# A written order for the ramp of a one-core attention block: load, norm, transposes and first projection

## The chip, the cores and the metric

One core of a Trainium2 chip runs the whole program. The metric is device time in microseconds (us), median of several runs of the same program; lower is better. Engines: PE (TensorE, products and transposes), DVE (VectorE), ACT (ScalarE), POOL (GpSimd), SP (its queue issues the large DMAs).

## The reference

One layer over x of 256 tokens by 1024, fp32:

```python
h = rmsnorm(x, norm_mix)
proj = h @ w_in                       # 9 * 512 + 8 + 3 * 1024 columns
q_a, k_a, v_a, q_b, k_b, v_b, f_b, q_c, k_c, v_c, g = split(proj)
o_a = stick_breaking_attention(q_a, k_a, v_a)      # 8 heads of 64 each
o_b = forgetting_attention(q_b, k_b, v_b, f_b + b_forget)
o_c = moba_attention(q_c, k_c, v_c, alibi slopes)  # one block here: causal + ALiBi
mixed = sum_n sigmoid(g[n]) * (o_n @ w_branch[n])
x = x + mixed @ w_out
x = x + relu(rmsnorm(x, norm_mlp) @ w_up) ** 2 @ w_down
return rmsnorm(x, norm_final)
```

Every product is made to near fp32 precision from halves: each operand is split into a rounded part "hi" (type fp32r) and the rest "lo" = value - hi, and three products hi\*hi, lo\*hi and hi\*lo are added up in PSUM.

## The kernel before, in words

The weights (75.5 MB by their shapes) stream through SBUF in 1 MB units, listed in `plan` (L72 to L83) in the order of use: q, k, v of branch a, and so on, then gates, lifts, out, up, down. `pump` (L88) converts them: for each unit one DMA into a "raw" buffer (two of these, tag `raw`; SP queue, L95), then in halves hi = copy (ACT, L107) and lo = raw - hi (DVE, L110). Up to 7 halves lie ahead of their use (`HALVES`); `used` (L117) counts a half as consumed and pumps the next. The first unit, q of branch a, is an exception: its halves are two DMAs of 512 KB (`raw0`, L103), and its hi parts `whi_qa` are made on POOL (L109), lo of half 0 on DVE and lo of half 1 on POOL (L110).

Before the first product the kernel loads x (two tiles of 128 tokens, L154) and runs 12 products on zeros (`pw`, L172). Each tile is normalised: sum of squares on ACT and DVE (L185, L186), power -1/2 on POOL (`rstd`, L199), scaling to `h` on DVE and ACT (L224, L225). PE transposes the 16 128x128 blocks (`ptr`, L205), and each of the 8 blocks of features k becomes, times the norm's gain, `hT`: hi by ACT (L210) and lo by DVE (L212). Constants for the attention masks are made on POOL and DVE (L240 to L269): `zeros`, `minus`, `neg_past`, `neg_tri`, `neg_ones` (a cast on DVE, L249), `identr` (L251), `rel`, `sel`, `neg_sel`, `ones_row`.

`proj_first` (L306) makes q of branch a: 48 products of 128x128 by 256 columns into two PSUM tiles (j = 0, 1), in six runs of 8 over k, named (j, a, b): a picks hi or lo of the weights, b hi or lo of `hT`. Order: (0,0,0), (1,0,0), (0,1,0), (0,0,1), (1,0,1), (1,1,0). `qk_split` (L281) then writes q as hi and lo into zero-padded tiles (`pad_hi`, `pad_lo`). After it come k of branch a (`proj_qk`, 48 products), the 16 products `pf` of the forget gate (`forget_terms`, L435; weights `raw_f` and `wf`), v of branch a (`proj_v`), and the rest: attention steps interleaved with further projections, gates, lifts, output projection, MLP.

What sets the order of instructions: the text goes through a planner, which simulates the program with costs of its own and lists the instructions of each engine as they come ready in its simulation; each engine then executes its list in order. So the order on an engine need not be that of the text: L249 and L251 are written behind L212 and run ahead of it on DVE.

Of the kernel before, what the change touches and what calls it, by code (L numbers as in the profile page):

```python
# [24 lines left out]
EPS = 1e-6  # L25
WARM = 12
LO = 32
ROOT_D = 32.0
# [9 lines left out]
def hybrid_attention_block(ctx, tc, x, norm_mix, w_in, b_forget, w_branch, w_out,  # L38
# [48 lines left out]

    def pump():  # L88
        while state["next"] < min(2 * len(plan), state["used"] + HALVES):
            n, i = divmod(state["next"], 2)  # L90
# [8 lines left out]
            if n:  # L99
                raw = state["raw"][part]  # L100
            else:
                raw = act.tile([P, a, b], F32, name="raw0", tag=("v_hi", "v_lo")[i], bufs=2)
                nc.sync.dma_start(raw, src[part])  # L103
            hi = wp.tile([P, a, b], F32R, name=f"whi_{which}{br}{j}{i}", tag="whi", bufs=HALVES)
# [12 lines left out]
    def used(n=1):  # L117

        state["used"] += n
        pump()  # L120
# [40 lines left out]

    ident = const.tile([P, P], F32, name="ident")
    make_identity(nc, ident)
    minus_half = const.tile([P, 1], F32, name="minus_half")
    nc.gpsimd.memset(minus_half, -0.5)

# [7 lines left out]

    pg = ps.tile([P, 2 * KD], F32, name="pg", tag="dense", bufs=3)
    nc.tensor.transpose(pg, gains, ident[0:2 * KD, 0:2 * KD])
    g_col = const.tile([P, 2 * KD], F32, name="g_col")
    nc.vector.tensor_scalar(g_col[:, 0:KD], pg[:, 0:KD], ROOT_D, None, op0=ALU.mult)
    nc.vector.tensor_copy(g_col[:, KD:], pg[:, KD:])
    g_mix, g_mlp = g_col[:, 0:KD], g_col[:, KD:2 * KD]  # L180

    def square_sum(src, junk, ss):

        n = src.shape[-1] // 2
        nc.scalar.activation(junk[:, 0:n], src[:, 0:n], AF.Square, accum_out=ss[:, 0:1])  # L185
        nc.vector.tensor_tensor_reduce(junk[:, n:], src[:, n:], src[:, n:], 1.0, 0.0, ALU.mult, ALU.add, ss[:, 1:2])  # L186

    def total_square(src, junk, so_far=D * EPS):


        ss = small.tile([P, 2], F32, name="ss", tag="ss")
        square_sum(src, junk, ss)
        total = small.tile([P, 1], F32, name="total", tag="total")
        made = nc.vector.scalar_tensor_tensor(total, ss[:, 0:1], so_far, ss[:, 1:2], op0=ALU.add, op1=ALU.add)
        return total, made

    def rsqrt(ms):
        rstd = small.tile([P, 1], F32, name="rstd", tag="rstd")
        nc.gpsimd.tensor_tensor(rstd, ms, minus_half, op=ALU.pow)  # L199
        return rstd  # L200

    def transposes(h, t, k0, pt):

        for i in range(2):
            nc.tensor.transpose(pt[:, i, t], h[:, (k0 + i) * P:(k0 + i + 1) * P], ident)  # L205

    def split_gain(pt, k0, g, hi, lo):
        src = [pt[:, i].rearrange("p t q -> p (t q)") for i in range(2)]
        for i, k in enumerate((k0, k0 + 1)):
            nc.scalar.activation(hi[:, k], src[i], AF.Copy, scale=g[:, k:k + 1])  # L210
        for i, k in enumerate((k0, k0 + 1)):
            nc.vector.scalar_tensor_tensor(lo[:, k], src[i], g[:, k:k + 1], hi[:, k].bitcast(F32),  # L212
                                           op0=ALU.mult, op1=ALU.subtract)

    def ptr(tag):
        return ps.tile([P, 2, NT, P], F32, name="ptr", tag=tag, bufs=3 if tag == "dense" else None)

    hT = keep.tile([P, KD, 2, S], F32R, name="hT", tag="hT")
    h_hi, h_lo = hT[:, :, 0], hT[:, :, 1]
    hs = []  # L220
    for t in range(NT):
        h = act.tile([P, D], F32, name="h", tag="pad_lo", bufs=2)
        rstd = rsqrt(total_square(x_sb[t], h)[0])
        nc.vector.tensor_scalar(h[:, 0:512], x_sb[t][:, 0:512], rstd, None, op0=ALU.mult)  # L224
        nc.scalar.activation(h[:, 512:], x_sb[t][:, 512:], AF.Copy, scale=rstd)  # L225
        hs.append(h)
    for k0 in range(0, KD, 2):
        pt = ptr("po" if k0 == 2 else "dense")
        for t in range(NT):
            transposes(hs[t], t, k0, pt)  # L230
        split_gain(pt, k0, g_mix, h_hi, h_lo)
    pump()


# [27 lines left out]
    sel = act.tile([LO, H, P], F32, name="sel", tag="v_hi", bufs=2)  # L262
    nc.gpsimd.memset(sel, -1.0)
    neg_sel = act.tile([LO + H, H, P], F32R, name="neg_sel")
    for j, n in ((0, LO), (LO, H)):
        nc.gpsimd.affine_select(neg_sel[j:j + n], sel[0:n], pattern=[[1, H], [0, P]], compare_op=ALU.is_equal,
                                fill=0.0, base=0, channel_multiplier=-1)
    ones_row = act.tile([H, S], F32, name="ones_row")
    nc.gpsimd.memset(ones_row, 1.0)  # L269


# [21 lines left out]
    def proj_qk(which, br, quad):  # L293

        padded = (which == "q") == (br == "a")
        for j in range(2):
# [7 lines left out]
            yield  # L304

    def proj_first():  # L306
# [162 lines left out]
    def forget_bias(pair):  # L469
# [3 lines left out]
        for s in range(2):  # L473
            h = 2 * pair + s
            nc.tensor.matmul(pb[:, s], neg_sel[:, h], parts, start=True, stop=True)
        for s in range(2):
# [254 lines left out]
```

## Time and profile before

| | us |
|---|---|
| median of 3 runs | 471.01 (469.85 to 471.64) |
| profiled execution, time | 471.74 |
| its span, first to last instruction | 470.0 |
| PE busy in the span | 456.7 (97%) |
| DVE busy | 328.2 (70%) |
| ACT busy | 274.1 (58%) |
| POOL busy | 42.1 (9%) |
| mean granted PE clock | 0.993 of full speed |

Times in the profile are from the start of the span. An engine's row merges neighbouring instructions of one kind: its length is that of the merged stretch, and in brackets stands the idle time ahead of it and whose end ended it. Busy time of PE is modelled and pipelined: products overlap, so the distance between their starts is what counts. Matmuls run at 2.4 GHz where the granted clock is 1.00 and at 1.2 GHz where it is 0.50.

### The profile page before, as it was taken

The page shows a single profiled execution, that of the slowest core. Times are in us where ns is not written, and L with a number is a line of the kernel's source. Part 1 is how long each engine was busy: PE and PEld are TensorE (multiplying, and loading weights), DVE is VectorE, ACT ScalarE, POOL GpSimd, SP SyncE. Part 2 cuts the span into 40 slices and gives each one's busy share as a digit, 9 for nine tenths or more (in the row PEclk, how much of TensorE's full clock was granted, in tenths as well). Part 3 has the DMA queues.
Part 4 walks back from the last instruction along what each step waited for, and adds up shares of the span by engine and source line. Part 5 has one row for each costly group of instructions (what it writes and reads, how often), then busy time and mean ns, then how long its engine had stood idle before and what let it go on. Part 6 is the DMA issues. An engine that isn't in the chain of part 4 may idle for free. (4 is left out here: it accounts for less than half of the span.)

```text
span 470.0 us, 6865 instructions
## 1 busy us (share of the span) xinstructions
PE 456.7 (97%) x2583; PEld 394.9 (84%) x2583; DVE 328.2 (70%) x544; ACT 274.1 (58%) x474; POOL 42.1 (9%) x79
## 2 busy tenths in 40 slices
PE   6999999999999999999999998999999999999993
PEld 3888998899899888888888887888888888888882
DVE  3987787778878877758858848987788744444425
ACT  6358898777767696556556436566555543334302
POOL 3910111132100001000000000000000000000012
PEclk9899999999999999999999999999999999999998
DMA  8377344343345448655555626776665555555202
GB/s 287 86 263 259 119 157 146 122 142 129 120 149 164 139 144 276 217 181 179 181 180 179 190 79 189 223 214 184 186 196 200 201 199 178 181 178 179 90 1 89
DMA packets 56834, 79.65 MB, mean 169 GB/s; under 512 B 2385, under 2 KB 44641, under 8 KB 56801
## 3 DMA queue, kind: packets, MB, share of 16 engines
q1 hardware_dynamic: 56464, 78.81, 52.0%
q8 instruction: 20, 0.33, 0.3%
q10 hardware_dynamic: 336, 0.40, 0.2%
q14 instruction: 14, 0.11, 0.1%
HBM read 78.16 MB, written 1.05 MB: 169 GB/s over the span
## 5 line engine op out<-in xcount | busy, mean ns | idle before, releaser
L110 DVE TENSOR_TENSOR wlo_d<-raw,whi_d 128x1024 fp32r<-128x1024 f32 x32 | 39.2, 1226 | 41.5 <-ACT whi_d L107 41.5
L136 PE MATMUL pu<-h,whi_u 128*128 128x512 f32 x256 | 64.7, 393 | 1.2 <-DVE h L212 1.2
L107 ACT ACTIVATE whi_d<-raw 128x1024 fp32r<-128x1024 f32 x32 | 33.9, 1061 | 50.5 <-PE ptok L136 42.4
L136 PEld LDWEIGHTS pu<-h,whi_u 128*128 128x128 f32 x256 | 45.9, 189 | 9.8 <-DVE h L212 1.5
L107 ACT ACTIVATE whi_u<-raw 128x1024 fp32r<-128x1024 f32 x32 | 33.5, 1060 | 29.7 <-PE pu L136 14.8
L136 PE MATMUL ptok<-whi_d,u_lo 128*128 128x512 f32 x128 | 50.5, 395 | 0.0
L136 PE MATMUL ptok<-whi_d,u_hi 128*128 128x512 f32 x128 | 50.5, 395 | 0.0
L110 DVE TENSOR_TENSOR wlo_u<-raw,whi_u 128x1024 fp32r<-128x1024 f32 x32 | 39.0, 1223 | 15.4 <-ACT whi_u L107 15.3
L136 PE MATMUL pg<-hT,whi_g 128*128 128x512 f32 x192 | 48.3, 393 | 0.0
L136 PEld LDWEIGHTS pg<-hT,whi_g 128*128 128x128 f32 x192 | 34.6, 189 | 6.4
L136 PEld LDWEIGHTS pu<-h,wlo_u 128*128 128x128 f32 x256 | 35.2, 190 | 2.6
L110 DVE TENSOR_TENSOR wlo_g<-raw,whi_g 128x1024 fp32r<-128x1024 f32 x24 | 29.3, 1222 | 10.8 <-ACT whi_g L107 9.9
L136 PE MATMUL ptok<-wlo_d,u_hi 128*128 128x512 f32 x128 | 36.9, 395 | 0.0
L136 PE MATMUL pu<-h,wlo_u 128*128 128x256 f32 x256 | 36.0, 282 | 0.0
L107 ACT ACTIVATE whi_g<-raw 128x1024 fp32r<-128x1024 f32 x24 | 25.4, 1058 | 12.1 <-PE pg L136 4.8
L136 PEld LDWEIGHTS ptok<-whi_d,u_hi 128*128 128x128 f32 x128 | 24.1, 188 | 5.6
L136 PEld LDWEIGHTS ptok<-wlo_d,u_hi 128*128 128x128 f32 x128 | 24.1, 188 | 5.6
L136 PEld LDWEIGHTS ptok<-whi_d,u_lo 128*128 128x128 f32 x128 | 24.1, 188 | 5.6
L136 PEld LDWEIGHTS pg<-hT,wlo_g 128*128 128x128 f32 x192 | 26.2, 190 | 1.9
L689 POOL TENSOR_TENSOR xg<-x,g_fin 128x512 f32<-128x512 f32 x2 | 2.9, 1474 | 268.6 <-issue 267.2
L136 PE MATMUL pg<-hT,wlo_g 128*128 128x256 f32 x192 | 26.8, 282 | 0.0
L110 DVE TENSOR_TENSOR wlo_b<-raw,whi_b 128x1024 fp32r<-128x1024 f32 x12 | 14.7, 1224 | 10.4 <-ACT whi_b L107 10.3
(500 smaller groups left out, 952.7 us busy)
## 6 DMA issues: line engine op xcount, KB each, us to landing
raw<-in_w_in_dram SPq DMA_DIRECT2D x29, 1024.0 KB, 5.0
raw<-in_w_up_dram SPq DMA_DIRECT2D x16, 1024.0 KB, 5.6
raw<-in_w_down_dram SPq DMA_DIRECT2D x16, 1024.0 KB, 4.8
raw<-in_w_branch_dram SPq DMA_DIRECT2D x6, 1024.0 KB, 4.9
raw<-in_w_out_dram SPq DMA_DIRECT2D x4, 1024.0 KB, 4.8
x_sb<-in_x_dram SPq DMA_DIRECT2D x2, 512.0 KB, 3.8
raw<-in_w_in_dram SPq DMA_DIRECT2D x2, 512.0 KB, 7.7
x<-in_x_dram SPq DMA_DIRECT2D x2, 512.0 KB, 3.5
```

Source lines behind the costliest of these rows:

```text
L107: nc.scalar.activation(hi, raw, AF.Copy)
L110: (nc.gpsimd if n == 0 and i else nc.vector).tensor_tensor(lo, raw, hi.bitcast(F32), op=ALU.subtract)
L136: nc.tensor.matmul(o, l, r, start=first and i == 0, stop=last and i == len(pairs) - 1, **kw)
L689: nc.gpsimd.tensor_tensor(xg[:, d], x1[:, t, d], g_fin[:, d], op=ALU.mult)
```

## The change

`tc.manual_schedule()` opens a region from the table load to the end of `proj_first`. In it each engine issues its instructions in the order of the text; the order between engines, and where instructions from outside the region fall between them, stay the planner's. The text inside is put into a new order with it:

- both `raw0` DMAs are written right behind the two x DMAs (SP);
- the constants (`zeros` to `ones_row`, with the casts `neg_ones` and `identr` on DVE) come ahead of the sums of squares, and so ahead of `rstd` on POOL; `sel` and `neg_sel` go to the end of the region (`selectors`);
- the two scalings of h follow both sums of squares; the gain columns `g_col` come behind them;
- all 16 transposes, then all eight hi of `hT` (ACT), then the conversion of the two q halves, then all eight lo of `hT` (DVE);
- `proj_first` makes the first three runs of products for k = 0 to 3 first, then the same for k = 4 to 7 interleaved, then hi\*lo alternating between j = 0 and 1, and (1,1,0) last;
- the two halves of k (`pump(4)`) are converted inside the region ahead of `qk_split`; everything from `used(2)` on (v and later weights) is outside.

```diff
-    def pump():
-        while state["next"] < min(2 * len(plan), state["used"] + HALVES):
+    def pump(up_to=None):
+        while state["next"] < min(2 * len(plan), state["used"] + HALVES, up_to or 2 * len(plan)):
...
-                raw = act.tile([P, a, b], F32, name="raw0", tag=("v_hi", "v_lo")[i], bufs=2)
-                nc.sync.dma_start(raw, src[part])
+                raw = first_raw[i]
...
+    ramp = ExitStack()
+    ramp.enter_context(tc.manual_schedule())
     nc.scalar.preload_act_table_set("natural_log_exp_and_others")
     x_sb = [act.tile([P, D], F32, name="x_sb", tag=tag, bufs=2) for tag in ("v_hi", "v_lo")]
     for t in range(NT):
         nc.sync.dma_start(x_sb[t], x[t * P:(t + 1) * P])
+    first_raw = [act.tile([P, KD, P], F32, name="raw0", tag=tag, bufs=2) for tag in ("v_hi", "v_lo")]
+    for i in range(2):
+        nc.sync.dma_start(first_raw[i], plan[0][3][0][:, :, i * P:(i + 1) * P])
...
+    def gain_hi(pt, k0, g, hi):
+        for i, k in enumerate((k0, k0 + 1)):
+            nc.scalar.activation(hi[:, k], pt[:, i].rearrange("p t q -> p (t q)"), AF.Copy, scale=g[:, k:k + 1])
+
+    def gain_lo(pt, k0, g, hi, lo):
+        for i, k in enumerate((k0, k0 + 1)):
+            nc.vector.scalar_tensor_tensor(lo[:, k], pt[:, i].rearrange("p t q -> p (t q)"), g[:, k:k + 1],
+                                           hi[:, k].bitcast(F32), op0=ALU.mult, op1=ALU.subtract)
...
+    for t in range(NT):
+        hs.append(act.tile([P, D], F32, name="h", tag="pad_lo", bufs=2))
+        rstds.append(rsqrt(total_square(x_sb[t], hs[t])[0]))
+    for h, x_, rstd in zip(hs, x_sb, rstds):
+        nc.vector.tensor_scalar(h[:, 0:512], x_[:, 0:512], rstd, None, op0=ALU.mult)
+        nc.scalar.activation(h[:, 512:], x_[:, 512:], AF.Copy, scale=rstd)
...
+    pts = []
+    for k0 in range(0, KD, 2):
+        pt = ptr("po" if k0 == 2 else "dense")
+        for t in range(NT):
+            transposes(hs[t], t, k0, pt)
+        pts.append(pt)
+    state["raw"] = None
+    for k0 in range(0, KD, 2):
+        gain_hi(pts[k0 // 2], k0, g_mix, h_hi)
+    for i in range(2):
+        pump(i + 1)
+    for k0 in range(0, KD, 2):
+        gain_lo(pts[k0 // 2], k0, g_mix, h_hi, h_lo)
...
     def proj_first():
 
         qkv["q", "a", 0] = qk_tiles(True)
         w = [weights("q", "a", 0, j) for j in range(2)]
         p_ = [ps.tile([P, S], F32, name="pqk", tag="s2", bufs=2) for j in range(2)]
-        for j, a, b in ((0, 0, 0), (1, 0, 0), (0, 1, 0), (0, 0, 1), (1, 0, 1), (1, 1, 0)):
-            terms(p_[j], [(w[j][a][:, k], hT[:, k, b]) for k in range(KD)], (a, b) == (0, 0), (a, b) == (j, 1 - j))
-        used(2)
+        order = [(0, 0, 0, k) for k in range(4)] + [(0, 1, 0, k) for k in range(4)] + [(1, 0, 0, k) for k in range(4)]
+        order += [(j, a, 0, k) for k in range(4, KD) for j, a in ((0, 0), (0, 1), (1, 0))]
+        order += [(j, 0, 1, k) for k in range(KD) for j in range(2)] + [(1, 1, 0, k) for k in range(KD)]
+        for j, a, b, k in order:
+            nc.tensor.matmul(p_[j], w[j][a][:, k], hT[:, k, b], start=(a, b, k) == (0, 0, 0),
+                             stop=(a, b, k) == (j, 1 - j, KD - 1))
+        pump(4)
         for j in range(2):
             qk_split(p_[j], j, qkv["q", "a", 0], True, SCALE)
+        neg_sel.append(selectors())
+        ramp.close()
+        used(2)
```

## Rows read from the trace of the kernel before

**Rows 1.** Windows, three stretches: start:end, length, busy us (instructions) per engine, clock, DMA, GB/s

```profile
8.93:20.41 11.48, 8.90 (x51) 7.70 (x49) 9.32 (x13) 6.12 (x12) 10.92 (x14) 0.85 0.51 171
20.41:36.00 15.59, 15.59 (x102) 14.17 (x101) 12.93 (x20) 8.50 (x15) 4.66 (x11) 1.00 0.69 221
36.00:470.00 434.00, 424.91 (x2408) 369.50 (x2406) 302.94 (x501) 254.78 (x441) 24.28 (x45) 1.00 0.51 166
```

**Rows 2.** Waits of PE from 36 us on: us in total, times, longest

```profile
PE pu L136 <- DVE h L212: 1.2, 1, 1.2
PE pqk L136 <- DVE pad_lo L289: 0.8, 1, 0.8
```

**Rows 3.** Timeline of PE: start, us, what, count [idle before <- releaser]

```profile
10.03 0.50 PE L136 MATMUL pqk<-hT,whi_qa 128*128 128x256 f32 x2 [0.89 <-POOL whi_qa L109]
12.19 2.82 PE L136 MATMUL pqk<-hT,whi_qa 128*128 128x256 f32 x14 [1.66 <-POOL whi_qa L109]
...
16.42 3.19 PE L136 MATMUL pqk<-hT,whi_qa 128*128 128x256 f32 x16
19.45 1.12 PE L136 MATMUL pqk<-hT,wlo_qa 128*128 128x256 f32 x8
20.41 2.08 PE L136 MATMUL pqk<-hT,whi_ka 128*128 128x256 f32 x16
...
26.17 2.03 PE L136 MATMUL pf<-hT,wf 128*40 128x256 f32 x16
```

**Rows 4.** Timeline of DVE, the same columns

```profile
10.01 1.23 DVE L110 TENSOR_TENSOR wlo_qa<-raw,whi_qa 128x1024 fp32r<-128x1024 f32 x1 [2.24 <-POOL whi_qa L109]
12.32 2.41 DVE L249 CAST neg_ones<-minus 128x128 fp32r<-128x128 f32 x1 [1.08 <-POOL minus L243]
...
15.00 3.21 DVE L212 SCALAR_TENSOR_TENSOR hT<-ptr,g_col,hT 128x256 fp32r<-128x256 f32 x8
18.14 3.38 DVE L110 TENSOR_TENSOR wlo_ka<-raw,whi_ka 128x1024 fp32r<-128x1024 f32 x2
...
24.38 0.20 DVE L442 TENSOR_TENSOR wf<-raw_f,wf 128x64 fp32r<-128x64 f32 x1
```

**Rows 5.** Timeline of POOL, the same columns

```profile
1.32 0.29 POOL masks.py:199 TENSOR_SCALAR_AFFINE_SELECT ident<-ident 128x128 f32<-128x128 f32 x1
5.28 0.55 POOL L199 TENSOR_TENSOR rstd<-total,minus_half 128x1 f32<-128x1 f32 x1 [3.66 <-DVE total L194]
...
10.49 1.65 POOL L109 TENSOR_SCALAR whi_qa<-raw 128x1024 fp32r<-128x1024 f32 x1 [0.51 <-DMA raw<-in_w_in_dram]
...
12.25 2.39 POOL L110 TENSOR_TENSOR wlo_qa<-raw,whi_qa 128x1024 fp32r<-128x1024 f32 x1
14.58 0.42 POOL L237 TENSOR_SCALAR_AFFINE_SELECT neg_past<-zeros 128x256 fp32r<-128x256 f32 x1
...
17.33 3.11 POOL L266 TENSOR_SCALAR_AFFINE_SELECT neg_sel<-sel 32x1024 fp32r<-32x1024 f32 x2
```

**Rows 6.** Timeline of ACT, the same columns

```profile
8.30 3.03 ACT L210 ACTIVATE hT<-ptr,g_col 128x256 fp32r<-128x256 f32 x8 [0.30 <-PE ptr L205]
13.02 2.00 ACT L107 ACTIVATE whi_ka<-raw 128x1024 fp32r<-128x1024 f32 x2 [1.69 <-DMA raw<-in_w_in_dram]
...
26.55 2.01 ACT L107 ACTIVATE whi_va<-raw 128x1024 fp32r<-128x1024 f32 x2 [1.28 <-DMA raw<-in_w_in_dram]
```

**Rows 7.** Timeline of the SP queue, the same columns

```profile
8.72 0.79 SPq L438 DMA_DIRECT2D raw_f<-in_w_in_dram  x1
21.54 2.64 SPq L95 DMA_DIRECT2D raw<-in_w_in_dram  x2
```

**Rows 8.** Windows around the fall of the granted clock, columns as in rows 1

```profile
9.50:12.88 3.38, 1.19 (x7) 0.99 (x8) 1.79 (x2) 1.83 (x6) 2.87 (x4) 1.00 1.07 398
12.88:16.29 3.41, 3.41 (x18) 3.41 (x17) 3.41 (x6) 2.00 (x2) 3.41 (x8) 0.50 0.45 119
```

**Rows 9.** Timeline of PE, 13.55 to 14.7 us

```profile
13.32 1.70 PE L136 MATMUL pqk<-hT,whi_qa 128*128 128x256 f32 x7
```

More of the change, by code (lines that the diff above doesn't have):

```diff
@@ L159, in hybrid_attention_block @@
     nc.scalar.dma_start(bf_col, bass.AP(tensor=b_forget.tensor, offset=b_forget.offset, ap=[[1, H], [1, 1]]))
[L162 to L165, printed above, removed]
     idle = act.tile([P, 512], mybir.dt.bfloat16, name="idle", tag="sp", bufs=2)
@@ L172, in hybrid_attention_block @@
         nc.tensor.matmul(pw, idle[:, 0:P], idle, start=True, stop=True)
[L175 to L232, printed above, removed]
+    ident = const.tile([P, P], F32, name="ident")
+    make_identity(nc, ident)
+    minus_half = const.tile([P, 1], F32, name="minus_half")
+    nc.gpsimd.memset(minus_half, -0.5)
     def selected(name, shape, src, pattern, op, fill, step):
@@ L260, in hybrid_attention_block @@
                                 base=0, channel_multiplier=1)
[L262 to L267, printed above, removed]
     ones_row = act.tile([H, S], F32, name="ones_row")
@@ L269, in hybrid_attention_block, with square_sum, total_square @@
     nc.gpsimd.memset(ones_row, 1.0)
+    def square_sum(src, junk, ss):
+        n = src.shape[-1] // 2
+        nc.scalar.activation(junk[:, 0:n], src[:, 0:n], AF.Square, accum_out=ss[:, 0:1])
+        nc.vector.tensor_tensor_reduce(junk[:, n:], src[:, n:], src[:, n:], 1.0, 0.0, ALU.mult, ALU.add, ss[:, 1:2])
+    def total_square(src, junk, so_far=D * EPS):
+        ss = small.tile([P, 2], F32, name="ss", tag="ss")
+        square_sum(src, junk, ss)
+        total = small.tile([P, 1], F32, name="total", tag="total")
+        made = nc.vector.scalar_tensor_tensor(total, ss[:, 0:1], so_far, ss[:, 1:2], op0=ALU.add, op1=ALU.add)
+        return total, made
@@ new lines, in rsqrt, with transposes @@
+    def rsqrt(ms):
+        rstd = small.tile([P, 1], F32, name="rstd", tag="rstd")
+        nc.gpsimd.tensor_tensor(rstd, ms, minus_half, op=ALU.pow)
+        return rstd
+    def transposes(h, t, k0, pt):
+        for i in range(2):
+            nc.tensor.transpose(pt[:, i, t], h[:, (k0 + i) * P:(k0 + i + 1) * P], ident)
+    def gain_hi(pt, k0, g, hi):
+        for i, k in enumerate((k0, k0 + 1)):
+            nc.scalar.activation(hi[:, k], pt[:, i].rearrange("p t q -> p (t q)"), AF.Copy, scale=g[:, k:k + 1])
@@ new lines, in gain_lo, with split_gain, ptr @@
+    def gain_lo(pt, k0, g, hi, lo):
+        for i, k in enumerate((k0, k0 + 1)):
+            nc.vector.scalar_tensor_tensor(lo[:, k], pt[:, i].rearrange("p t q -> p (t q)"), g[:, k:k + 1],
+                                           hi[:, k].bitcast(F32), op0=ALU.mult, op1=ALU.subtract)
+    def split_gain(pt, k0, g, hi, lo):
+        gain_hi(pt, k0, g, hi)
+        gain_lo(pt, k0, g, hi, lo)
+    def ptr(tag):
+        return ps.tile([P, 2, NT, P], F32, name="ptr", tag=tag, bufs=3 if tag == "dense" else None)
@@ new lines, in hybrid_attention_block @@
+    hT = keep.tile([P, KD, 2, S], F32R, name="hT", tag="hT")
+    h_hi, h_lo = hT[:, :, 0], hT[:, :, 1]
+    hs = []
+    rstds = []
+    for t in range(NT):
[4 more added lines that the diff above has]
+        nc.scalar.activation(h[:, 512:], x_[:, 512:], AF.Copy, scale=rstd)
@@ new lines, in hybrid_attention_block @@
+    pg = ps.tile([P, 2 * KD], F32, name="pg", tag="dense", bufs=3)
+    nc.tensor.transpose(pg, gains, ident[0:2 * KD, 0:2 * KD])
+    g_col = const.tile([P, 2 * KD], F32, name="g_col")
+    nc.vector.tensor_scalar(g_col[:, 0:KD], pg[:, 0:KD], ROOT_D, None, op0=ALU.mult)
+    nc.vector.tensor_copy(g_col[:, KD:], pg[:, KD:])
+    g_mix, g_mlp = g_col[:, 0:KD], g_col[:, KD:2 * KD]
+    pts = []
[4 more added lines that the diff above has]
+        pts.append(pt)
@@ L272, in qk_tiles @@
+    state["raw"] = None
+    for k0 in range(0, KD, 2):
+        gain_hi(pts[k0 // 2], k0, g_mix, h_hi)
+    for i in range(2):
+        pump(i + 1)
+    for k0 in range(0, KD, 2):
+        gain_lo(pts[k0 // 2], k0, g_mix, h_hi, h_lo)
     def qk_tiles(padded):
@@ L304, in proj_qk, with selectors @@
             yield
+    neg_sel = []
+    def selectors():
+        sel = act.tile([LO, H, P], F32, name="sel", tag="v_hi", bufs=2)
+        nc.gpsimd.memset(sel, -1.0)
+        made = act.tile([LO + H, H, P], F32R, name="neg_sel")
+        for j, n in ((0, LO), (LO, H)):
+            nc.gpsimd.affine_select(made[j:j + n], sel[0:n], pattern=[[1, H], [0, P]], compare_op=ALU.is_equal,
+                                    fill=0.0, base=0, channel_multiplier=-1)
+        return made
     def proj_first():
@@ L474, in forget_bias @@
             h = 2 * pair + s
-            nc.tensor.matmul(pb[:, s], neg_sel[:, h], parts, start=True, stop=True)
+            nc.tensor.matmul(pb[:, s], neg_sel[0][:, h], parts, start=True, stop=True)
         for s in range(2):
```

## The prediction

> **What bounds the kernel now.** I read the windows first. From 20.41 us PE is never idle to 36 us (15.59 of 15.59 busy), and from there to the end it is busy for 424.91 of 434.00 us [rows 1]; of the 9.09 us that are missing, its waits make 2.0 [rows 2], and the rest is the tail behind the last product. From 20.41 us on, then, the run is one queue of products, and the moment at which the k projection starts sets the end. In the stretch before it, 8.93 to 20.41, PE is busy for 8.90 of 11.48 us at a mean clock of 0.85 [rows 1]. So I went on to the timeline of PE there, then to the engine that ends each pause.
>
> PE starts two products at 10.03, waits 1.66 us for `whi_qa` and restarts at 12.19; from 16.42 its sixteen products hi\*lo stretch over 3.03 us (to 19.45), where eight others take 0.96 (19.45 to 20.41) [rows 3]. Those sixteen wait for DVE: `hT` lo begins at 15.00, one part every (3.21 - 0.47) / 7 = 0.39 us (0.47 being one pass), the last ending at 18.21 [rows 4]. All its inputs lay there at 8.30 + 3.03 = 11.33 [rows 6]; DVE was free at 11.24 but had the cast `neg_ones` ahead, which waited for `minus` and then took 2.41 us beside POOL's 2.39 us `wlo_qa` [rows 4, 5]. The chain is: cast, lo of `hT`, hi\*lo products, (1,1,0), k projection.
>
> **Two prices.** At full clock, products of 256 columns follow each other every (20.41 - 19.45) / 8 = 0.12 us [rows 3]; a restart after a pause costs 0.10 more, since the second product at 10.03 begins 0.50 - 0.28 = 0.22 after the first (0.28 is one product's length). At half clock seven take 1.70 us of which the last is 0.42: (1.70 - 0.42) / 6 = 0.213 each [rows 9].
>
> **The change, part by part.**
>
> *Up to the first product: nothing.* The `raw0` DMAs keep their place behind x on SP. The constants now stand ahead of `rstd` on POOL. From `neg_past` to the start of `neg_sel` they and the memset of `sel` take 17.33 - 14.58 = 2.75 us [rows 5], and `minus` comes on top (about 0.2). Started behind `ident` at 1.32 + 0.29, they end by 4.6 us, while `rstd` has its input at 5.28 [rows 5]. Without those 0.7 us of cover each late us would be one on the path. The two casts fall into DVE's wait for x. `g_col` now comes behind both scalings of h: I take 0, since ACT makes the first four hi of `hT` by 8.30 + 3 x 0.36 + 0.48 = 9.86 and PE wants them at 10.03 [rows 3, 6]; being later than that by 0.2 would cost the excess.
>
> *The products.* (0,0,0) for k = 0 to 3 starts at 10.03 as before and now runs its four to 10.6. (0,1,0) needs `wlo_qa` of half 0: 10.01 + 1.23 = 11.24 [rows 4]. (1,0,0) needs `whi_qa` of half 1: 10.49 + 1.65 = 12.14 [rows 5], so PE restarts at 12.19 as before, with 8 of the 48 products done in place of 2. The other 40 need 0.22 + 39 x 0.12 = 4.90 us and would end at 17.09 if nothing is late. The lo of `hT` follow `wlo_qa` on DVE at 11.24 and end at 11.24 + 3.21 = 14.45; the first product with lo stands behind 16 of the 40, at 12.19 + 0.22 + 15 x 0.12 = 14.2, the last at 16.0: no wait. `wlo_qa` of half 1 is done on POOL at 14.64 [rows 5] and wanted at 16.1. So the k projection starts at 17.09 in place of 20.41: **3.32 us saved**, of which 0.1 per restart is already counted.
>
> *What is late next.* The k halves: ACT makes `whi_ka` from 13.02 to 15.02, bound by its DMA [rows 6]; DVE makes `wlo_ka` behind the lo of `hT`, from 14.64 for 2 x 1.23 to 17.1, the first half at 15.9 against its use at 17.09 + 16 x 0.12 = 19.0. Then `pf` at 26.17 - 3.32 = 22.85 [rows 3], which needs `wf` from DVE. Behind `wlo_ka` DVE has four `pad_lo` (about 0.4 each) and the first two lo of v (2.46): 21.2. The `neg_sel` of POOL now meets these: before it met `wlo_ka`, and that pair took 3.38 us in place of 2.46 [rows 4, 5], so 0.92 more: 22.1, then `wf` 0.20. Slack 0.5 us; I take 0 and keep up to 1 us of loss. The next weights: SP issued their DMA at 21.54 when `wlo_ka` was done, and it landed by 26.55 [rows 6, 7]. It now goes out at 17.1, 4.4 us earlier, with PE only 3.3 earlier. From there on every stage moves as a whole, and the tail is the same.
>
> *The clock.* It fell to 1.2 GHz at 12.88 and came back at 16.29 [rows 8]. Before the fall PE had two products between pauses of 0.89 and 1.66 us [rows 3]; ahead of the rise it worked without a pause. In the old kernel this cost next to nothing, because the lo of `hT` came later still. In the new one it would lie on the path. Ends: no fall, 3.32 saved. The same fall at the same place: five products from 12.19 to 12.88, then 3.41 / 0.213 = 16 slow ones, then 19 x 0.12 = 2.28, k projection at 18.57, 1.84 saved. All 40 slow: 12.19 + 0.22 + 39 x 0.213 = 20.72, 0.31 lost. I take no fall, narrowly: eight products now break up the time from 10.03 to 12.19, and no pause is over 0.75.
>
> The Trainium skill (TensorE: Matmul & The Clock Gate, section Why this matters for your kernels) warns of long pauses between bursts of products alone; by that rule neither kernel would lose its clock here, and the time would be the forecast's. The trace disagrees: the old kernel lost it after two short pauses [rows 3, 8].
>
> **The sum.** In the profiled execution (471.74 us, span 470.0) 471.74 - 3.32 = 468.4. This execution is 0.73 over the median of the three runs, 471.01; from the median it is **467.7 us**.
>
> **Rivals.**
> - *The clock falls as before.* For it: the pauses are shorter but still there. Against: four times as many products by 12.19. 471.01 - 1.84 = 469.2.
> - *The lo of `hT` are held up by POOL's `wlo_qa` as the cast was.* They would run from 14.64, the last ending at 17.85; then a restart of 0.22 and the remaining nine products, 1.08: k projection at 19.2, 1.2 saved, 469.8. For it: the cast ended with POOL's operation. Against: eight lo passes ran at an even 0.39 us beside POOL's selects [rows 4, 5]. By the Trainium skill (SBUF — State Buffer, section Who interferes with whom) a DVE instruction with at most one SBUF input, outside the fast modes, does not meet POOL; these read PSUM and one SBUF tile, and the rows agree.
> - *The saving is used up behind the region.* If the planner puts `wf` behind the third and fourth lo of v, these wait for the DMA of 17.1, ready some 5 us later, then 3.4 us for both (26.55 to the end of the last lo on DVE, about 30.0, before): 25.6, `pf` at 25.8, 0.4 saved, 470.6. Part of that is likelier than all.
> - *Slower: `raw_f` falls behind the weight DMAs on SP.* It went out at 8.72, long before the DMA of 21.54, although the text has it behind that [rows 7]. The planner lists the SP queue anew. Behind the second DMA that waits for a free buffer it would go out at about 22, and behind the third at about 26; with 5 us to land and 0.5 to convert, `pf` starts at 31.5, 5.3 later than before: 476.3. It decides from an issue at 20.7 on, where `pf` misses the old 26.17. Against: nothing makes `raw_f` ready later than before.
> - *The region changes little*, the planner's order on the path being kept: 471.0. Against: the text's order on DVE and PE plainly differs from the one in the rows.
>
> **Chances.** Forecast 0.49, clock 0.27, lo held up 0.06, used up behind the region 0.07, no effect 0.03, `raw_f` 0.04; 0.04 for a larger saving, should the old kernel's other runs lose more to the clock than the profiled one. A measurement of this kernel can tell about 0.5% (2.4 us) from no change: faster means below 468.6. The forecast's own range, 467.7 with 0.9 either way for the uncertain wait at `pf` and the spread between runs, puts 0.43 of its 0.49 there; with 0.05 of the clock's case and the larger saving: faster 0.52. Slower (over 473.4): `raw_f` and a little for a bad new plan, 0.06. Same: 0.42. The range, 466.6 to 470.5, holds the forecast, nearly all of the clock's case and the lo's; the forecast's own is 466.8 to 468.6.
>
> **What would show it.** In the new profile: eight products before 12.2 and no pause of PE between 12.2 and the k projection; `neg_ones` and `identr` done before 4.1; lo of `hT` from about 11.2 to 14.5 at 0.39 each; k projection at 17.1 (18.6 with a low clock from about 12.9); `pf` at 22.9 directly behind k; PE busy throughout from there. I am wrong if PE waits at `pf` or v, if the clock is low over most of the 40 products, or if the stage behind 36 us has more than the old 2.0 us of waits.

## The result and the profile after

The changed kernel takes **466.15 us** (median of 4, 465.81 to 467.42), the kernel before 470.91 beside it (469.85 to 471.64): a ratio of 0.9906, interval 0.9879 to 0.9933. The forecast was 467.7, range 466.6 to 470.5. The direction and the main step were right; the gain is 4.8 us in place of 3.3, and the time lies 0.45 below the range.

The profiled execution of after took 467.42 us (span 465.7), so it is one of its slowest. Windows of its ramp, of the time to 36 us, of the rest (this window reaches 4.3 us past the end of the span), and of the stretch with a low clock (columns as in [rows 1]), against [rows 1, 8]:

```profile
8.08:17.49 9.41, 8.93 (x62) 8.93 (x63) 8.62 (x16) 8.22 (x15) 8.86 (x9) 0.82 0.75 241
17.49:36.00 18.51, 18.51 (x114) 16.42 (x112) 13.47 (x21) 10.52 (x16) 5.00 (x6) 1.00 0.71 229
36.00:470.00 434.00, 421.41 (x2395) 367.11 (x2394) 300.63 (x499) 253.15 (x438) 24.44 (x45) 0.99 0.51 164
9.07:12.49 3.42, 3.42 (x19) 3.42 (x18) 3.04 (x6) 3.41 (x9) 3.06 (x3) 0.50 1.08 396
```

From the k projection at 17.49 on, PE is busy throughout as before, and of the two waits of [rows 2] one is left:

```profile
PE pu L135 <- DVE h L238: 1.2, 1, 1.2
```

PE, for [rows 3]: no wait is left between the transposes and `pf`.

```profile
8.56 2.80 PE L230 MATMUL ptr<-ident,h 128*128 128x128 f32 x14 [0.49 <-DVE h L256]
11.02 1.20 PE L337 MATMUL pqk<-hT,whi_qa 128*128 128x256 f32 x4
12.02 0.85 PE L337 MATMUL pqk<-hT,wlo_qa 128*128 128x256 f32 x4
...
14.49 2.20 PE L337 MATMUL pqk<-hT,whi_qa 128*128 128x256 f32 x17
16.53 1.12 PE L337 MATMUL pqk<-hT,wlo_qa 128*128 128x256 f32 x8
17.49 2.08 PE L135 MATMUL pqk<-hT,whi_ka 128*128 128x256 f32 x16
...
23.25 2.03 PE L135 MATMUL pf<-hT,wf 128*40 128x256 f32 x16
```

DVE, for [rows 4]: the cast `neg_ones`, 2.41 us before, takes 0.41 far ahead of POOL's weight work; lo of `hT` follows `wlo_qa` at once.

```profile
2.00 0.41 DVE L192 CAST neg_ones<-minus 128x128 fp32r<-128x128 f32 x1 [0.81 <-POOL minus L186]
...
9.45 1.22 DVE L109 TENSOR_TENSOR wlo_qa<-raw,whi_qa 128x1024 fp32r<-128x1024 f32 x1 [0.79 <-POOL whi_qa L108]
10.59 3.22 DVE L238 SCALAR_TENSOR_TENSOR hT<-ptr,g_col,hT 128x256 fp32r<-128x256 f32 x8
13.72 2.57 DVE L109 TENSOR_TENSOR wlo_ka<-raw,whi_ka 128x1024 fp32r<-128x1024 f32 x2
...
19.72 0.21 DVE L471 TENSOR_TENSOR wf<-raw_f,wf 128x64 fp32r<-128x64 f32 x1
```

POOL for [rows 5] and SP for [rows 7]: `whi_qa` starts at 8.08 (8.93 before), `raw_f` keeps its early place, and the third weight load goes out 1.17 us ahead of the k projection, where before it went out 1.13 behind it.

```profile
8.08 1.34 POOL L108 TENSOR_SCALAR whi_qa<-raw 128x1024 fp32r<-128x1024 f32 x1
...
11.66 2.41 POOL L109 TENSOR_TENSOR wlo_qa<-raw,whi_qa 128x1024 fp32r<-128x1024 f32 x1
```
```profile
7.74 0.86 SPq L467 DMA_DIRECT2D raw_f<-in_w_in_dram  x1
16.32 39.96 SPq L95 DMA_DIRECT2D raw<-in_w_in_dram  x9
```

**The two profiled executions add up.** Spans 470.0 and 465.7. `whi_qa` begins 0.85 us earlier: in before POOL waited 1.68 us for the transfer of `raw0` there, in after it came straight from `rstd` of the second tile. This start differs by execution (7.50 to 8.93 in five profiles of before). From there to k it is 9.41 in place of 11.48: 2.07. From k to the end of PE it is 441.15 in place of 442.55: 1.40. Sum 4.32, the difference of the spans. So this pair of profiles alone does not give the forecast's 3.32 anywhere; it took further executions to see it.

### The profile page after: what moved, and what is told of

It is laid out like the page before. It is cut to its first block, busy times and chain, and to the rows that moved or that the text cites. A ratio compares the mean times of both kernels' runs of the same rounds, so it can differ in the third digit from the quotient of the medians.

```text
span 465.7 us, 6866 instructions
## 1 busy us (share of the span) xinstructions
PE 454.4 (98%) x2583; PEld 394.4 (85%) x2583; DVE 325.8 (70%) x544; ACT 275.3 (59%) x474; POOL 43.0 (9%) x79
## 5 line engine op out<-in xcount | busy, mean ns | idle before, releaser
L109 DVE TENSOR_TENSOR wlo_u<-raw,whi_u 128x1024 fp32r<-128x1024 f32 x32 | 39.0, 1224 | 15.2 <-ACT whi_u L106 14.7
L109 DVE TENSOR_TENSOR wlo_b<-raw,whi_b 128x1024 fp32r<-128x1024 f32 x12 | 14.7, 1225 | 10.4 <-ACT whi_b L106 10.3
```

The lines of the kernel that those rows point to most:

```text
L109: (nc.gpsimd if n == 0 and i else nc.vector).tensor_tensor(lo, raw, hi.bitcast(F32), op=ALU.subtract)
```

## The experiments

In the times below, an execution is called one with a fall when its mean granted clock is 0.994 or less, and one without from 0.995 on: in all 20 profiles here the first kind has a stretch at 1.2 GHz before 21 us, the second has none. The interval behind a median is that of its ratio to the kernel before on the same chip. Gaps between k and `whi_qa` are from the start of the first POOL `whi_qa` to the first k product.

### Where the ramp's gain comes from

**b_no_cast**: the kernel before, with one line changed.
```diff
-    nc.vector.tensor_copy(neg_ones, minus)
+    nc.gpsimd.memset(neg_ones.bitcast(F32), -1.0)
```


> The kernel before with one instruction less on DVE: neg_ones is filled by a POOL memset instead of the DVE cast; every other order is as before. Theory A (the cast keeps the lo of hT back, and an earlier third weight DMA removes the 0.81 us wait of PE at 52.4 us): lo of hT starts near 11.3 in place of 15.0, sixteen hi*lo products in about 1.9 us in place of 3.03, k projection near 17.8 at full clock and near 19.3 with a fall of the clock like the old one; the DMA that went out at 21.5 goes out at about 17.5 to 18, and the wait at 52.4 shrinks or goes; total 1.5 to 3.5 us faster. Rival B (POOL's wlo_qa holds up the lo passes as it did the cast): lo of hT from 14.6, under 1 us faster.

468.86 us (467.68 to 470.62), ratio 0.9965 (0.995 to 0.9979). On DVE lo of `hT` starts 3.2 us behind the start of `whi_qa` (8.20), where before it was 6.07:

```profile
10.42 1.07 DVE L251 CAST identr<-ident 128x128 fp32r<-128x128 f32 x1
11.40 3.21 DVE L212 SCALAR_TENSOR_TENSOR hT<-ptr,g_col,hT 128x256 fp32r<-128x256 f32 x8
14.53 2.34 DVE L110 TENSOR_TENSOR wlo_ka<-raw,whi_ka 128x1024 fp32r<-128x1024 f32 x2
```

So one cast, off every list of dear instructions, is worth about two fifths of the whole change: 1.83 us between the medians, 1.90 between executions without a fall (467.86 against 469.76). Its PE also waits 0.57 for `wf` at 25 us, which takes part of it back.

**a_text_only** (after without the region) and **a_old_products** (after with the six runs of eight products):
```diff
-    ramp.enter_context(tc.manual_schedule())
```
```diff
-        order = [(0, 0, 0, k) for k in range(4)] + [(0, 1, 0, k) for k in range(4)] + [(1, 0, 0, k) for k in range(4)]
...
+        order = [(j, a, b, k) for j, a, b in ((0, 0, 0), (1, 0, 0), (0, 1, 0), (0, 0, 1), (1, 0, 1), (1, 1, 0)) for k in range(KD)]
```


> The changed text without the region: the planner orders it. Its lists put both casts behind the sums of squares, ahead of the scalings of h, and one product of half 1 fourth on PE. Theory A: it keeps most of the gain, since the casts are still ahead of the lo of hT: k projection 0.5 to 1.0 us later than with the region, total about 466.5 to 467.5. Rival: the region itself is what counts, 469 or more.

> The changed kernel with the six runs of eight products in the old order, inside the region. By my sum eight products are done before whi_qa of half 1 in either order, so 0 to 0.3 us slower than the changed kernel if the clock behaves alike. Rival: the new order keeps the clock up, and without it the k projection is about 1.5 us later.

466.52 (0.9898 to 0.9927) and 466.43 (the same interval): 0.3 to 0.4 us above after, which the intervals do not tell from nothing. The trace of a_text_only tells more. A product of half 1 stands fourth on PE and waits 0.91 us for `whi_qa`, and k starts 8.77 us behind the start of `whi_qa` (7.68) in place of 8.16 (after_timed, below; both without a fall), so the region is worth 0.6 us in the ramp, as was expected; an earlier `whi_qa` hides most of it in this execution's time.

```profile
9.22 0.83 PE L336 MATMUL pqk<-hT,whi_qa 128*128 128x256 f32 x3
10.96 0.50 PE L336 MATMUL pqk<-hT,whi_qa 128*128 128x256 f32 x2 [0.91 <-POOL whi_qa L108]
...
16.45 1.72 PE L135 MATMUL pqk<-hT,whi_ka 128*128 128x256 f32 x13
```

For the order of the products there is no such row, since the one profile of a_old_products has a fall: its executions without one have a median of 466.36, 0.27 above those of after. **b_region**, the old text held in a region, is the counterpart:
```diff
+    ramp = ExitStack()
+    ramp.enter_context(tc.manual_schedule())
...
-        used(2)
...
+        ramp.close()
+        used(2)
```


> The text of the kernel before, with the region around it and used(2) behind it, nothing moved: does the region alone do it? On DVE the lo of hT then stand ahead of wlo_qa of half 0, and the casts far behind. Theory A: the lo of hT are done by 12, but wlo_qa of half 0 comes behind them and meets POOL's wlo_qa of half 1, so it is late (about 13 to 15) and PE fills in with early k products; k's last product 1.5 to 2.5 us earlier than before, total 467.5 to 469. Rival (the region by itself is the gain): 466 to 467.

471.13 (470.7 to 472.41; ratio 1.0021, 1.0007 to 1.0035): slower by 0.2%, and neither of the times expected. In the old text the norm of tile 1 stands behind the scaling of tile 0; PE waits 2.45 and 2.28 us for `h` where the planner had let both sums go first:

```profile
8.10 0.69 PE L207 MATMUL ptr<-ident,h 128*128 128x128 f32 x2 [2.45 <-DVE h L226]
11.07 3.25 PE L207 MATMUL ptr<-ident,h 128*128 128x128 f32 x14 [2.28 <-DVE h L226]
```

The clock has a part in it: it is at 0.50 from 7.58 to 14.40 us, twice as long as in any other profile here, and all ten executions have a mean clock of 0.990 or less. How the loss divides between the waits and the clock is not shown.

So most of the gain comes with the new text. Of its parts only the cast was tested by itself; that lo of `hT` then meets nothing on DVE is what the rows show of the rest.

**a_rows** halves `raw0` by rows (pieces of 1 KB in place of 512 bytes) and converts it in pieces of 512 elements.
```diff
-    first_raw = [act.tile([P, KD, P], F32, name="raw0", tag=tag, bufs=2) for tag in ("v_hi", "v_lo")]
+    first_raw = [act.tile([P, KD // 2, 2 * P], F32, name="raw0", tag=tag, bufs=2) for tag in ("v_hi", "v_lo")]
...
-        nc.sync.dma_start(first_raw[i], plan[0][3][0][:, :, i * P:(i + 1) * P])
+        nc.sync.dma_start(first_raw[i], plan[0][3][0][:, 4 * i:4 * i + 4])
...
+                rows = [(slice(4 * h, 4 * h + 4), first_raw[h][:, :, i * P:(i + 1) * P]) for h in range(2)]
+                for r, raw in rows:
+                    nc.gpsimd.tensor_scalar(hi[:, r], raw, 1.0, 0.0, op0=ALU.mult, op1=ALU.add)
```


> The changed kernel with the halves of the first raw load cut by rows k 0 to 3 and 4 to 7 (pieces of 1 KB in place of 512 bytes) and its conversions cut the same way, four on POOL of 512 elements for each of hi and of the second half's lo. If the landing of this load (about 7.4 to 8.9 us from execution to execution) sets the first conversion and with it the ramp, whi_qa and wlo_qa start about 0.5 to 1 us earlier, the first k product is at 14.5 to 15.8 in place of 16.4, and the time is 464.6 to 465.7. Rival (POOL behind the statistics, or ACT's hi of hT, sets the ramp and not the landing): the first k product at 16.0 to 16.6 and 466.0 to 466.6. Rival on the other side (two pieces behind each conversion make the first product wait for both halves): first k product after 17, 467 or more.

466.16 (465.89 to 467.7): the first rival's time, no gain. Half 0 of q now needs both transfers, and the second lands no earlier with larger pieces: POOL converts from it at 9.68 (9.75 in after_timed), so `wlo_qa` ends later and lo of `hT` begins at 11.34 in place of 10.30; k at 16.12 in place of 16.24.

```profile
8.32 0.62 POOL L109 TENSOR_SCALAR whi_qa<-raw 128x512 fp32r<-128x512 f32 x1 [1.12 <-DMA raw<-in_w_in_dram]
9.68 2.21 POOL L109 TENSOR_SCALAR whi_qa<-raw 128x512 fp32r<-128x512 f32 x3 [0.74 <-DMA raw<-in_w_in_dram]
```

### How far the executions differ

**before_again**, **before_p1**, **before_p2**, **before_p3**, **after_again** are the two kernels unchanged, one execution each; **after_timed** is after, timed six times.

> The kernel before once more, for a second profile: it tells what of the profiled execution belongs to the kernel. If the wait of 0.81 us at 52.4 and the k projection at 20.4 belong to it, both are there again (k within 19.5 to 20.5, since x and raw0 may land up to 1 us earlier). If they were chance, the wait is gone.

> The changed kernel once more, for a second profile. My sum puts the k projection at 17.1 with the old landing time of raw0 (8.93) and no fall of the clock; shifted by the landing of this execution it should be 8.2 us behind the start of whi_qa of half 0 if the clock stays up, 9.7 us behind it if it falls while products run. The first profile had 9.4 with a fall at 9.07. No PE wait near 50.

> One more profile of the kernel before, for what its slower executions (470.5 and above) carry that the faster ones (469.1 to 470.1) do not. By the theory of the lead: the wait of a pads product near 50 us (some 1.0 us between the last z product and the q product of branch b beyond the 3.8 us without it), with k to the end of PE at 442.3 to 442.6 in place of 441.2. By the theory of the clock: a fall in the ramp that moves the first k product from 11.5 to 12.5 or more behind the start of whi_qa, with 441.2 behind it. An execution of the faster kind has neither.

> As before_p1, another execution: if it is one of the slower kind (470.5 and above), the theory of the lead wants the wait near 50 us in it, the theory of the clock a later first k product.

> As before_p1, another execution: if it is one of the slower kind (470.5 and above), the theory of the lead wants the wait near 50 us in it, the theory of the clock a later first k product.

> The changed kernel unchanged, timed on the same chip as the two beside it: 466.0 to 466.8. By the theory of the lead, one execution in ten or fewer is at 467.5 or above (the wait near 50 us), where the kernel before has more than half of its executions at 470.5 or above. If the wait were as frequent here as before, the times would fall into two groups some 1.2 us apart in like shares.

| execution | time | clock low from | start of `whi_qa` | k behind it | k to end of PE |
|---|---|---|---|---|---|
| before | 471.74 | 12.88 | 8.93 | 11.48 | 442.55 |
| before_again | 469.60 | none | 8.07 | 11.50 | 441.25 |
| before_p1 | 469.71 | 12.66 | 8.17 | 11.48 | 441.25 |
| before_p2 | 470.80 | 17.61 | 7.50 | 13.07 | 441.45 |
| before_p3 | 470.70 | 16.91 | 7.59 | 13.09 | 441.24 |
| after | 467.42 | 9.07 | 8.08 | 9.41 | 441.15 |
| after_again | 467.93 | none | 8.46 | 8.16 | 442.53 |
| after_timed | 466.15 | none | 8.08 | 8.16 | 441.13 |

This table is the answer. Without a fall, k starts 11.50 behind `whi_qa` in before and 8.16 in after: 3.34, the forecast's 3.32. The clock was misjudged. A fall at 12.7 or 12.9 costs before nothing, as the prediction said of its one profile; but in two of five profiles it comes at 16.91 or 17.61, when lo of `hT` is done or nearly so (17.10, 17.08), and then 1.6 us of it lie on the path. The whole times of these two are only 1.1 us longer (470.80 and 470.70 against 469.60 and 469.71), since `whi_qa` began some 0.5 us earlier in them; whether an early start and a late fall go together, five profiles can't tell. `whi_qa` on POOL and k on PE in after_timed:

```profile
8.08 1.04 POOL L108 TENSOR_SCALAR whi_qa<-raw 128x1024 fp32r<-128x1024 f32 x1 [0.71 <-DMA raw<-in_w_in_dram]
16.24 1.00 PE L135 MATMUL pqk<-hT,whi_ka 128*128 128x256 f32 x7
```

before_again and before_p2, POOL and PE:

```profile
8.07 1.05 POOL L109 TENSOR_SCALAR whi_qa<-raw 128x1024 fp32r<-128x1024 f32 x1 [0.58 <-DMA raw<-in_w_in_dram]
...
14.69 4.08 PE L136 MATMUL pqk<-hT,whi_qa 128*128 128x256 f32 x16 [0.47 <-DVE hT L212]
18.61 1.12 PE L136 MATMUL pqk<-hT,wlo_qa 128*128 128x256 f32 x8
19.57 2.08 PE L136 MATMUL pqk<-hT,whi_ka 128*128 128x256 f32 x16
```
```profile
7.50 1.32 POOL L109 TENSOR_SCALAR whi_qa<-raw 128x1024 fp32r<-128x1024 f32 x1
...
14.40 4.67 PE L136 MATMUL pqk<-hT,whi_qa 128*128 128x256 f32 x16 [0.47 <-DVE hT L212]
18.86 1.91 PE L136 MATMUL pqk<-hT,wlo_qa 128*128 128x256 f32 x8
20.57 2.29 PE L136 MATMUL pqk<-hT,whi_ka 128*128 128x256 f32 x16
```

Eight products of (1,1,0) take 20.57 - 18.86 = 1.71 in place of 0.96, at a granted clock of 0.50 (before_p2, windows around the fall):

```profile
9.06:17.61 8.55, 6.71 (x38) 4.81 (x36) 7.46 (x12) 4.47 (x10) 8.30 (x13) 1.00 0.65 222
17.61:20.57 2.96, 2.96 (x16) 2.96 (x15) 2.96 (x3) 2.22 (x3) 2.81 (x4) 0.50 0.02 6
```

Of 90 timed executions of before, 61 have a fall: median 470.79, against 469.76 for the 29 without. Of 11 of after, 3 have one: 467.42, against 466.09. The profile that the prediction rests on also held the 0.8 us wait of [rows 2], as one other of the eight does, an execution of after:

```profile
49.04 2.14 PE L135 MATMUL pqk<-hT,whi_ka 128*128 128x256 f32 x16 [1.19 <-DVE pad_lo L299]
```

### What makes the clock fall

**a_fill** lays idle products on zeros into after's pauses, **b_fill** and **b_fill2** into those of before: b_fill ahead of 12.2 us alone, b_fill2 also one ahead of seven of the hi\*lo products, which come 0.39 us apart. (In b_fill ACT makes one `pad_hi` behind the first two hi of v and DVE's list is that of before. In b_fill2 the planner listed more anew than was expected: ACT's list differs at 16 places from 15 us on, DVE's at 22 from 23 us on, all but ACT's first two behind the start of k.)
```diff
+            for _ in range({(0, 0, 0, 0): 2, (0, 1, 0, 0): 3}.get((j, a, b, k), 0)):
+                nc.tensor.matmul(pw2, idle[:, 0:P], idle, start=True, stop=True)
```
```diff
+                for _ in range({0: 3, 2: 4}.get(n, 0)):
+                    nc.tensor.matmul(pw2, idle[:, 0:P], idle, start=True, stop=True)
```
```diff
+                fill = {0: 0, 2: 4}.get(n, 0) + (1 if b and j == 0 and k >= 1 else 0)
+                for _ in range(fill):
+                    nc.tensor.matmul(pw2[:, 0:512], idle[:, 0:P], idle[:, 0:512], start=True, stop=True)
```


> The changed kernel with idle products on zeros in PE's pauses: two more ahead of the transposes, two ahead of the first product, three ahead of (0,1,0). Theory: where the clock falls in the ramp (one in four timed executions of the changed kernel, about 1.3 us), this keeps it up: all executions within 0.7 us of each other at a mean clock of 0.995 or more, median 465.8 to 466.3. Rival: the idle products stand in the way and cost 0.3 to 0.6 us each time, or the clock falls all the same: 466.3 to 467.5.

> The kernel before with seven idle products on zeros laid into PE's two pauses ahead of 12.2 us (three ahead of its first product, four behind its second; 128 columns by 512 each), so that the clock should not fall there; DVE's list is that of before, ACT makes one pad_hi later. The third raw load stays about 1.1 us behind the first k product. Theory of the clock (the slower half of the executions of before has a fall of the clock in the ramp): the median is 469.0 to 469.8 in place of 470.7 and few executions are above 470.3. Theory of the lead (the wait near 50 us makes the slower half): the median stays at 470.2 to 470.9 with the same two groups, though the clock no longer falls.

> The kernel before with idle products on zeros (128 columns by 512): four behind PE's second product, and one ahead of each hi*lo product of (0,0,1) for k = 1 to 7, which wait for DVE's lo of hT 0.39 us apart; there PE then works nearly without a pause. DVE's list is that of before but for one exchange near 30 us, ACT makes one pad_hi later, as in b_fill. Theory (the fall of the clock that costs before 1.6 us comes out of this stretch): no or few executions with a mean clock of 0.991 to 0.993, the first k product 11.4 to 11.7 us behind the start of whi_qa, and a median of 469.4 to 470.0, against 470.77 for b_fill; what is left above 470.3 has the wait near 50 us. Rival (the clock falls whatever PE does there, or the slower executions are made by the wait alone): the median stays at 470.4 to 470.9. Rival on the other side (the idle products delay the hi*lo products): k 0.5 or more later and a median above 471.

a_fill: 466.35 (466.1 to 466.69), no fall in 6 of 6, which beside 3 of 11 can be chance, and no faster: k comes 0.15 us later than in after_timed (16.39 against 16.24), and in after few executions have a fall to save. b_fill: 470.77 (469.24 to 472.06), a fall in 6 of 12; the early pauses alone are not its cause, and with the clock falling all the same the run decides nothing on the lead. Where these six falls lie is not shown: the one profile of b_fill has none. b_fill2: no fall in 6 of 6, beside 9 of 11 in the kernel before on the same chip, and k 11.50 behind `whi_qa`, as expected; but the median is 471.78 (ratio 1.004, 1.0025 to 1.0055), since the new lists bring a wait of their own:

```profile
18.82 1.12 PE L321 MATMUL pqk<-hT,wlo_qa 128*128 128x256 f32 x8
19.77 2.08 PE L136 MATMUL pqk<-hT,whi_ka 128*128 128x256 f32 x16
...
29.97 1.19 PE L136 MATMUL pv<-whi_va,hT 128*128 128x512 f32 x4 [1.02 <-DVE qk_lo L289]
```

So the falls that are left with the early pauses filled go when the products 0.39 us apart, with idle time under 0.3 us between them, are filled too. By this the falls at 16.91 and 17.61 come from that stretch; those at 12.66 and 12.88 lie ahead of it, behind the early pauses. What the median of before would be without the stretch can't be read from b_fill2. The Trainium skill (TensorE: Matmul & The Clock Gate, section A second HAM failure mode: psum-queue depth-cycling) tells of a kernel in which short idle times between groups of products, often repeated, bring the clock down; these runs are in line with it, for products that wait singly. The rule that the prediction cited, long pauses alone, is the one that they contradict.

### The lead of the weight stream

Before the further profiles I took the earlier third load for the rest of the gain. **a_late_k** spends six spare passes on DVE ahead of `wlo_ka`; **a_sp_mid**, **a_sp_late** keep every list of PE, DVE, ACT and POOL and hold back that load by a small transfer ahead of it on SP, which reads `sel` (mid) or `neg_sel` (late); **a_sp_mid2** is a_sp_mid again.
```diff
+    spare = pts[3][:, 0].rearrange("p t q -> p (t q)")
+    for _ in range(6):
+        nc.vector.tensor_scalar(spare, spare, 1.0, None, op0=ALU.mult)
```
```diff
+        late = const.tile([LO, 1], F32, name="late")
+        state["late"] = nc.sync.dma_start(late, sel[:, 0, 0:1])
...
-                nc.sync.dma_start(state["raw"], src)
+                d = nc.sync.dma_start(state["raw"], src)
+                if n == 3:
+                    follow(d, state["late"])
```


> The changed kernel with six spare passes on DVE (128x256 in PSUM, written back unchanged) between the lo of hT and wlo_ka, about 2.4 us, so that the DMA of the third weight unit goes out that much later (near 18.7 in place of 16.3) while the k projection keeps its start. Theory A (the lead of this DMA over PE removed the wait at 52.4): PE waits again near 48.6, by 0.5 to 1.0 us, and the total is 0.5 to 1.2 us above the changed kernel. Rival C (the planner's new list or chance removed it): no new wait, within 0.3 us.

> The changed kernel with one more small transfer on SP's queue that reads neg_sel, and the third raw load ordered behind it; the lists of PE, DVE, ACT and POOL are those of the changed kernel. The third raw load then goes out at about 19 to 20 us in place of 16.3, so some 2.5 to 3.5 us after the k projection's first product (about 16.5) and no longer ahead of it. Theory (how far the weight stream leads PE decides whether the wait of a pads product for DVE's pad_lo near 50 us occurs): the wait, 1.0 to 1.5 us, is there in most executions, the stretch from the first k product to the end of PE is 442.2 to 443 in place of 441.1, and the median is 467.2 to 467.8. Rival (the wait comes and goes by the execution, whatever the lead): within 0.3 us of the changed kernel, 466.0 to 466.6. Rival (the stream has slack of several us there): no wait in the profile and the same time.

> As a_sp_late, with the small transfer reading sel, which POOL has filled at about 16.95 us: the third raw load then goes out at about 17.7, some 1.3 us after the first k product (16.3), which is the same lead of PE over the weight stream as in the kernel before (21.54 against 20.41: 1.13 us); all lists of PE, DVE, ACT and POOL are those of the changed kernel. Theory of the lead: the extra gain of the change beyond the 3.3 us of the ramp goes with it, so the times spread as those of the kernel before do, over some 2 us, with more than half of them 0.8 us or more above the fastest, and the median is 466.9 to 467.6, 0.7 to 1.4 above the changed kernel's 466.16. Rival (not the lead but another difference of the two lists makes the wait near 50 us rare in the changed kernel): 466.0 to 466.5, with one in ten or fewer above 467.5.

> One more profile of a_sp_mid, whose slower executions (467.5 to 468.1) had a mean clock of 0.995 to 0.998 and so hardly a fall in the ramp. Theory of the lead: an execution at 467.3 or above without a fall in the ramp has a wait of PE between 40 and 55 us (a projection's product that waits for DVE's pad_lo or v_lo) of 0.8 us or more, and 442.3 us or more from the first k product to the end of PE. Rival: no such wait, and the time goes elsewhere.

a_late_k (466.36; 0.9896 to 0.9933) is no test of the lead alone, since the planner listed part of v ahead of `pf` anew. With that list a late load costs nothing: it goes out at 18.18, 2.4 us behind k (15.82), the profile has no wait of PE from k on but the 1.2 us for `h` of [rows 2], and the two executions without a fall take 465.85 and 465.87. a_sp_late: 468.93 (467.95 to 470.06), more than expected; the load goes out at 19.53 (16.04 in after_timed), and PE waits, at another place than expected:

```profile
18.82 0.60 SPq L346 DMA_DIRECT2D late<-neg_sel  x1
19.53 39.36 SPq L95 DMA_DIRECT2D raw<-in_w_in_dram  x9
```
```profile
41.42 2.18 PE L137 MATMUL pqk<-hT,whi_qa 128*128 128x256 f32 x16 [1.91 <-DVE v_lo L368]
```

Its executions without a fall have a median of 468.04, 1.95 over those of after: the 1.91 us of that wait. Eight of its twelve have a fall, against three of eleven of after; the runs give no reason. a_sp_mid (load at 17.60): 467.52 (466.39 to 468.07), within what was expected; 467.58 without a fall. With the lists of after the lead has a price, then: 1.5 us of it cost 1.4 us, 3.5 us cost 2.0, or 2.8 with the falls. Both profiles of a_sp_mid (466.73, 466.35) fell on executions whose clock fell during the transposes, which holds PE back behind the stream, and show no wait; where its other executions lose their 1.4 us stays unseen. Nor does the lead explain before: with about the same lead as a_sp_mid, only 7 of the 29 executions of before without a fall are over 470.5.

## Why the prediction was right and where it failed

*The k projection, 3.32 us saved: right.* 11.50 to 8.16 behind `whi_qa`, 3.34. The forecast's 17.09 - 8.93 = 8.16 was met to the last digit, which is more than its rounded terms could promise. Its parts hold too: lo of `hT` begins 2.2 us (10.30 - 8.08, after_timed) behind `whi_qa` (forecast 2.31), 0.39 us a pass beside POOL's `wlo_qa`, so the rival "lo held up by POOL" is out. The part whose value these runs can't tell from nothing is the order of the products (a_old_products, 0.27).

*Why the cast was dear: right.* It took 2.41 us and ended at 14.73, 0.09 behind POOL's `wlo_qa` (14.64); alone it took 0.41. In b_no_cast the cast `identr` took 1.07 beside POOL's `whi_qa` and again ended 0.09 behind it (11.49 and 11.40). The Trainium skill (SBUF — State Buffer, section Who interferes with whom) has casts among the operations that can take the port pair that DVE shares with POOL, and says that the loser waits for the whole instruction; these rows agree.

*`pf`, `raw_f`, "used up behind the region": right that nothing is lost.* `wf` is ready at 19.9, 3.3 us ahead of `pf`, and 2.3 ahead in after_timed (19.71, 22.00), without a fall; the forecast's 0.5 us of slack was too tight. `wlo_ka` was done 8.21 us behind the start of `whi_qa`, as worked out (17.1 - 8.93 = 8.2), but `wf` 11.85 behind it in place of 13.4: the 0.92 us for `neg_sel` on POOL did not come, since the lo of v beside it took 1.20 us and the one ahead of it 1.21, and one `pad_lo` fewer (0.4) stood ahead of `wf`.

*The clock as a rival, 1.84 saved: half right.* It falls in 3 of 11 executions of after (chance given 0.27; that they agree is luck), but at 9.07 in its profile, and at 7.72 to 8.23 in three of its variants, during the transposes, and costs 1.25 (9.41 - 8.16) in place of the 1.48 worked out, and 0.85 and 0.49 in a_sp_mid and a_sp_mid2 (9.01 and 8.65), whose products are those of after.

*The step that failed* is the sentence that in the old kernel the fall "cost next to nothing, because the lo of `hT` came later still", and with it the subtraction of 3.32 from the median of 471.01. It is true of the profiled execution, and was carried over to all of them. In 61 of 90 executions before has a fall, and those are 1.03 us slower in the median; after removes the stretch that brings it on at 17 us. The prediction did name this case, a larger saving "should the old kernel's other runs lose more to the clock than the profiled one", and gave it 0.04. By medians over all runs, 470.60 - 466.17 = 4.43: executions without a fall make 469.76 - 466.09 = 3.67 of it, and the medians lie 0.84 and 0.08 above these, 0.76. The fastest ever seen of each, 469.11 and 465.81, differ by 3.30. Of the 1.54 us between the forecast (471.01 - 3.32 = 467.69) and the measured 466.15, then, 0.76 are the falls, 0.35 (3.67 - 3.32) lie beyond the ramp, and 0.41 is chance: the median of three runs from which the forecast was taken off lay that much over the 470.60 of the 90.

*"From there on every stage moves as a whole": nearly.* The lists allow it: PE's are the same from the k projection on, DVE's and ACT's from 27.6 and 26.6 us of before on. Of the 3.67, some 0.3 are beyond the ramp. Without a fall the third load goes out 1.3 us earlier against PE than before (16.04 with k at 16.24, 20.71 with k at 19.57), which the prediction noted (4.4 against 3.3) and priced at nothing; by its times, a_sp_mid puts 1.4 on it in the changed kernel, though no trace shows where, and a_late_k, with another list, puts nothing. How much of the 0.3 it is, and how often the wait near 50 us occurs in either kernel, these runs leave open.

## What to carry to other kernels

Before a forecast is taken off a median, ask which kind of execution the profile is: the times of before lie in two groups, and one profile shows only one of them. An engine that is fed at an even but slow pace, here PE with a product every 0.39 us, can cost its clock a little later, so removing such a stretch can be worth more than its length. Look for the small instruction ahead of the chain that runs beside a long one of another engine: one cast of 128 by 128 was worth 1.8 us.

## What was not expected of the hardware

- The same two SP transfers of `raw0`, issued at the same time, let `whi_qa` start anywhere from 7.50 to 8.93 us in five executions of one kernel (at 7.50 POOL came straight from `rstd`, at 8.93 it had waited 1.68 us for the transfer); twice the piece size (a_rows) left the second one's first use at 9.68, against 9.75.
- The stretch at 1.2 GHz came at 12.88, 12.66, 17.61 and 16.91 us in four executions of the same program and not at all in a fifth. The Trainium skill (TensorE: Matmul & The Clock Gate, section What's actually happening) says of the slow products at a kernel's start that their number differs from run to run. Here the same holds for a stretch behind the start, and it decides 1.6 us of the ramp.
- A fall that comes early may even help: in a_sp_mid it held PE behind the weight stream (k at 16.98 and 16.80, against 16.24 in after_timed), and those two executions (466.73, 466.35) beat four of its five others (467.46 to 468.07; the fifth took 466.39). With so few this is a hint and not shown.
